# Attention weights turned by fp32 transposes instead of transposed logits; value products a step behind; projections spread evenly over two heads

## The chip, the core and the metric

The kernel runs on one core of a Trainium2 chip. The metric is the device time of one execution in microseconds. The kernel before took 1159.56 us, the median of three runs (1157.66 to 1160.25).

## The reference, cut to what matters

A trunk of two layers over a sequence of 1024 positions with 1024 channels, in float32. Layer 0 is a gated linear recurrence and is not touched here. Layer 1 is attention with a forget gate, 16 heads of 64 channels, causal:

```python
u = h @ w_in                       # q, k, v, gate and one forget logit per head
cum = cumsum(log_sigmoid(f_logit + b_f), axis=1)
logits = (q_blk @ k.T) / sqrt(64) + cum[query] - cum[key]
p = softmax(where(key <= query, logits, -1e30))
o = p @ v
y = (o * silu(gate)) @ w_out       # then the residual sum, and a last RMS norm
```

To hold float32 precision, the kernel splits every matmul operand into a high and a low part (type float32r) and sums three products: high with high, high with low, low with high.

## The kernel before, in words

**Stages.** Layer 0 takes up to some 425 us of the profile. Then come the norm, the first projections, and the attention, head by head, to about 1129 us. The output projection is done in part among heads 13 to 15 (`partial`, whose sums go through DRAM) and ends in `turned`, which turns the stream by fp32 transposes (L850), adds the last two pairs of heads (L854 to L856) and norms.

**One head.** `T[s]` and `U[s]` (`s` is the head's parity) hold k and q with their high and low parts, laid out so that two products give a logit: `T[:, 0]` with `U[:, 0]`, and `T[:, 1]` with `U[:, 1]`, where the second also carries the forget sums. `load` (L559) fills them by DMAs from the projection's tiles `qk`. Two generators then work on a head, each once for each half `c` of the queries:

- `maxima(hd, c)` (L631) makes the logits of 128 queries at a time with queries on the partitions (L654, L655), finds the masked row maximum on DVE (L659), and exponentiates in place in PSUM on ACT (L662), only for the row sums `sums`; the exponentials themselves are thrown away. Its last steps turn the negated maxima (`mrow`, L668) and write them into rows 96 to 99 of `U` (L669), so that the transposed logits come with the maximum subtracted; and they bring the reciprocal sums into row form through DRAM (L680 to L690).
- `weigh(hd, c)` (L701) makes the logits once more, transposed, with keys on the partitions: two key blocks `j` per step, two products each (`ST`, L723 and L724), at least 256 query columns wide. ACT exponentiates out of PSUM into `p` (L729, L732), POOL zeroes the triangle above the diagonal (L737), DVE makes the high part `ph` (L81) and the low part `pl` (L86), and TensorE multiplies both with v into `O` (L757, L758), in the same step. After the last step, ACT and DVE fold the two halves of `O` into `yo` (L762, L763).

`scale` and `gated` (POOL) multiply the output with the gate and the reciprocal sums.

**PSUM.** Eight banks: two buffers of one bank for the tag `g` (projections), two of one bank for `O`, two of two banks for `S`. The logits of `maxima` and the transposed logits of `weigh` both take their tiles from `S`.

**Order.** `run(order, weigh, maxima, fill)` (L786) reads a string: `0` takes a step of `weigh`, `1` a step of `maxima`, and a dot a step of `fill`, the projection for the next pair of heads: six products of 512 columns. A head has two such runs: the first with `weigh(hd, 0)` and `maxima(hd, 1)`, the second with `weigh(hd, 1)` and `maxima(hd + 1, 0)`. `LAG` holds a fill step behind a matmul of a few steps before. In between these edges a planner orders each engine's instructions by its own estimate of when they are ready. `ORDERS` gives even heads (and 12 to 14) 16 dots and the other odd heads 10. In an even head the fill is `kq_units`, k and q of the next pair (16 steps); in an odd head `g_units`, the gate (8 steps). Every fourth head is followed by `values`, products alone. Weights go from DRAM to `wf` (SP queue, L91), their high part is made on ACT (L75) and their low part on POOL (`wl`, L86).

The lines around the change:

Of the kernel before, what the change touches and what calls it, by code (L numbers as in the profile page):

```python
# [17 lines left out]
P = 128  # L18
# [9 lines left out]
ORDERS = (("1.10111.0.10.", "1.1010.1.0.1..10"), (".1101.1..00..11.", "111.0.0.0.11.01...."))  # L28
# [10 lines left out]
def trunk(ctx: ExitStack, tc: tile.TileContext, xt, w0, wg, wo0, pc, gn, gf, w1, wv, wf, bf, wo1, out):  # L39
# [65 lines left out]
    def gemm_steps(ps, pairs, chunks=(slice(0, HALF),)):  # L105

        pairs = list(pairs)
        for cs in chunks:
            o = ps[:, cs]
            for i, ((wh, wl), (xh, xl)) in enumerate(pairs):  # L110
                nc.tensor.matmul(o, wh, xh[:, cs], start=i == 0, stop=False)  # L111
                nc.tensor.matmul(o, wl, xh[:, cs], start=False, stop=False)  # L112
                nc.tensor.matmul(o, wh, xl[:, cs], start=False, stop=i == len(pairs) - 1)  # L113
                if i % 2:
                    yield

# [344 lines left out]
    with ExitStack() as l1:  # L461
# [4 lines left out]
        own = tu.tile([4, 4, P], BF16, name="own")  # L466
        nc.gpsimd.memset(own, 0.0)
        nc.gpsimd.affine_select(
            out=own, in_=own, pattern=[[1, 4], [0, P]], compare_op=ALU.not_equal, fill=1.0, base=0, channel_multiplier=-1
        )  # L470


# [9 lines left out]
        U = [tu.tile([P, 2, SEQ], F32R, tag=f"U{s}", name=f"U{s}") for s in range(2)]  # L482
        for s in range(2):
            nc.gpsimd.memset(f32(T[s][64:, 1]), 1.0)
            nc.vector.memset(f32(U[s][64:, 1]), 0.0)
            nc.vector.memset(f32(U[s][64:68, 1]), -1.0)

        def project(cb_i, use, hs=(0, 1)):

            w = list(weights(w1[cb_i]))  # L490
# [47 lines left out]
        def kq_units(pair, hs=(0, 1)):  # L538

            for is_k in (1, 0):  # L540
                if hs[0] == 0:
                    kq[pair, is_k] = tuple(
                        kqpool.tile([P, SEQ], F32R, tag=f"qk{p}{is_k}", name=f"qk{p}") for p in "hl"
                    )
                hi, lo = kq[pair, is_k]
                eng = nc.vector if pair == 0 else nc.scalar

                def use(h, pt):
                    cs = slice(h * HALF, (h + 1) * HALF)
# [7 lines left out]
                yield from project(is_k * 8 + pair, use, hs)  # L557

        def load(hd, cs=slice(0, SEQ)):  # L559
# [3 lines left out]
            for is_k, A in ((1, T[s]), (0, U[s])):  # L563
                hi, lo = (f32(z[rows, cs]) for z in kq[pair, is_k])
                nc.sync.dma_start(f32(A[:64, 0, cs]), hi)
                if is_k:
                    nc.sync.dma_start(f32(A[:64, 1, cs]), hi)
                    nc.sync.dma_start(f32(A[64:, 0, cs]), lo)
                else:
                    nc.sync.dma_start(f32(A[64:, 0, cs]), hi)  # L570
                    nc.sync.dma_start(f32(A[:64, 1, cs]), lo)
            nc.sync.dma_start(f32(T[s][66:68, 1, cs]), cumd[hd, :, cs])
            nc.sync.dma_start(f32(U[s][64:66, 1, cs]), cumd[hd, :, cs])


        drain(kq_units(0, (0,)))


# [4 lines left out]
        z = at.tile([HEADS, SEQ], F32, tag="p", name="z")  # L583
        e = at.tile([HEADS, SEQ], F32, tag="p", name="e")
# [3 lines left out]
        parts = [at.tile([HEADS, SEQ], F32R, tag=t, name="cp") for t in ("ph", "pl")]  # L588

        def forget(half):  # L590
# [4 lines left out]
            z_, e_, hi, lo = z[:, cs], e[:, cs], *(c[:, cs] for c in parts)  # L595
# [10 lines left out]
            for i in range(2):  # L606
                nc.sync.dma_start(cumd[:, i, cs], f32(parts[i][:, cs]))
            for hd in range(2):
                if half == 0:
                    load(hd, cs)  # L610
# [7 lines left out]
        def g_units(pair):  # L618
# [8 lines left out]
            yield from project(16 + pair, use)  # L627

        stats = {}

        def maxima(hd, c):  # L631

            pair, s = hd // 2, hd % 2
            if c == 0:
                stats[hd] = (
                    at.tile([P, 8], F32R, tag="st", name="st"),  # L640
                    at.tile([P, 8], F32, tag="sums", name="sums"),
                )
            st, sums = stats[hd]
            for i in range(4 * c, 4 * c + 4):
# [4 lines left out]
                qs = slice(i * P, n)  # L649
                for lo_, hi_ in ((0, min(n, HALF - o_)), (HALF - o_, n)):  # L650
# [3 lines left out]
                    nc.tensor.matmul(S[:, lo_:hi_], U[s][:, 0, qs], T[s][:, 0, lo_:hi_], start=True, stop=False)  # L654
# [364 lines left out]
```

## Time and profile before

| | |
|---|---|
| median of the runs | 1159.56 us |
| profiled execution | 1159.8 us, span 1157.9 us |
| TensorE busy | 1131.8 us, 98% of the span |
| VectorE (DVE) busy | 818.3 us, 71% |
| ScalarE (ACT) busy | 590.7 us, 51% |
| GpSimd (POOL) busy | 311.0 us, 27% |
| DMA | 105.41 MB, 31.9% of 16 engines |

A row of a group reads: line, engine, operation, output tile and input tiles, shapes, count, then busy time in us and the mean time of one in ns, then the idle time of the engine just before these instructions and what ended it. A row of the timeline reads: start in us, duration in us, engine, line, operation, tiles, shapes, count, and in brackets the idle time before with its releaser. A row by stretch reads: the stretch, its length, busy time and count of TensorE, of its weight loads, of DVE, ACT and POOL, then the granted clock, the DMA share and GB/s. A row of waits reads: who waited for whom, us in total, how many times, the longest. PEld are TensorE's weight loads. Matmuls are pipelined: the time shown for one is longer than the distance to the next.

### The profile page before, as it was taken

How to read it: one execution, taken by the hardware profiler on the slowest of the kernel's cores; microseconds unless marked ns; L12 is line 12 of the kernel's file. 1: busy time of each engine (PE TensorE's matmuls, PEld its weight loads, DVE VectorE, ACT ScalarE, POOL GpSimd, SP SyncE). 2: the span in 40 equal slices, each digit the busy share in tenths (PEclk: the TensorE clock that was granted, in tenths of full speed). 3: DMA queues.
4: the chain of work that ended last, by engine and by line, in shares of the span. 5: the costliest groups of instructions: out<-in, count | busy, mean ns of one | idle time of the engine just before them, and what ended most of it. 6: DMA issues, size and time to landing. Idle time of an engine off the chain costs nothing.

```text
span 1157.9 us, 15580 instructions
## 1 busy us (share of the span) xinstructions
PE 1131.8 (98%) x5565; PEld 944.8 (82%) x5565; DVE 818.3 (71%) x1294; ACT 590.7 (51%) x1009; POOL 311.0 (27%) x305
## 2 busy tenths in 40 slices
PE   9999999999999999999999999999999999999897
PEld 7787888888888887978888988889888898777685
DVE  7589766677566889556877757777577775577754
ACT  8388345345544656454554545545454454445323
POOL 1212212112021103342332333323333233141310
PEclk9999999999999999999999999999999999999898
DMA  6111111111111124351343323433234331646244
GB/s 211 51 41 50 51 51 55 42 50 41 51 59 37 55 73 151 98 142 38 92 120 92 92 64 92 120 92 83 65 92 110 92 84 60 182 138 202 80 159 182
DMA packets 60221, 105.41 MB, mean 91 GB/s; under 512 B 8744, under 2 KB 23720, under 8 KB 60144
## 3 DMA queue, kind: packets, MB, share of 16 engines
q1 hardware_dynamic: 60144, 104.42, 31.9%
q8 instruction: 44, 0.72, 0.3%
q14 instruction: 33, 0.27, 0.1%
HBM read 63.30 MB, written 15.93 MB: 68 GB/s over the span
## 4 chain that ended last, share of the span: by engine, by line
PE 47%; DVE 5%; ACT 2%; DMA 2%; issue 1%; POOL 1%; DVEq 0%; SPq 0%; ACTq 0%; POOLq 0%
PE gps L111 6%; PE gps L112 6%; PE gps L113 6%; PE O L758 3%; PE ST L723 3%; PE S L655 2%; PE S L654 2%; PE ST L724 2%; PE O L757 2%; PE vps L519 2%; PE vps L517 2%; PE vps L518 2%; DVE pl L86 2%; PE ops L112 1%; PE ops L113 1%
## 5 line engine op out<-in xcount | busy, mean ns | idle before, releaser
L86 POOL TENSOR_TENSOR wl<-wf,wh 128x512 fp32r<-128x512 f32 (+2 forms) x130 | 189.0, 1458 | 504.7 <-ACT wh L75 428.6
L111 PE MATMUL gps<-hh,wh 128*128 128x512 f32 x576 | 226.8, 394 | 1.1 <-DVE qkl L555 0.7
L113 PE MATMUL gps<-hl,wh 128*128 128x512 f32 x576 | 226.7, 394 | 0.0
L112 PE MATMUL gps<-hh,wl 128*128 128x512 f32 x576 | 226.7, 394 | 0.0
L75 ACT CAST wh<-wf 128x512 fp32r<-128x512 f32 (+2 forms) x156 | 94.0, 607 | 140.1 <-PE gps L113 43.1
L662 ACT ACTIVATE S<-S,st 128x128 f32<-128x128 f32 (+7 forms) x128 | 91.4, 714 | 114.0 <-DVE st L659 112.9
L113 PEld LDWEIGHTS gps<-hl,wh 128*128 128x128 f32 x576 | 108.3, 188 | 24.3 <-issue 0.2
L111 PEld LDWEIGHTS gps<-hh,wh 128*128 128x128 f32 x576 | 108.4, 188 | 22.6 <-DVE qkl L555 1.1
L112 PEld LDWEIGHTS gps<-hh,wl 128*128 128x128 f32 x576 | 108.5, 188 | 21.6 <-issue 0.5
L86 DVE TENSOR_TENSOR pl<-p,ph 128x512 fp32r<-128x512 f32 (+2 forms) x130 | 121.7, 953 | 2.3
L81 DVE CAST ph<-p 128x512 fp32r<-128x512 f32 (+2 forms) x130 | 79.2, 619 | 57.0 <-ACT p L729 30.2
L737 POOL TENSOR_SCALAR_AFFINE_SELECT p<-p 128x128 f32<-128x128 f32 (+1 forms) x128 | 47.5, 388 | 201.6 <-ACT p L729 98.1
L659 DVE CUSTOM_DVE_ANT_0 S<-S,mask 128x128 f32<-128x128 f32 (+7 forms) x128 | 96.6, 758 | 7.1 <-PE S L655 6.2
L351 DVE TENSOR_TENSOR x<-x,ops 128x512 f32<-128x512 f32 x80 | 54.0, 681 | 50.7 <-PE ops L113 50.6
L111 PE MATMUL ups<-hh,wh 128*128 128x512 f32 x192 | 76.3, 397 | 2.6 <-DVE us L261 1.9
L113 PE MATMUL ups<-hl,wh 128*128 128x512 f32 x192 | 75.9, 395 | 0.2
L112 PE MATMUL ups<-hh,wl 128*128 128x512 f32 x192 | 75.7, 394 | 0.3 <-POOL wl L86 0.3
L758 PE MATMUL O<-pl,v 128*128 128x512 f32 (+1 forms) x198 | 67.1, 348 | 7.8 <-DVE pl L86 7.8
L729 ACT ACTIVATE p<-ST 128x512 f32<-128x512 f32 (+1 forms) x68 | 53.0, 785 | 42.4 <-PE ST L724 35.5
L518 PE MATMUL vps<-wh,hl 128*128 128x256 f32 (+1 forms) x256 | 72.7, 285 | 0.0
L517 PE MATMUL vps<-wh,hh 128*128 128x256 f32 (+1 forms) x256 | 72.6, 285 | 0.0
L519 PE MATMUL vps<-wl,hh 128*128 128x256 f32 (+1 forms) x256 | 72.4, 284 | 0.0
(192 smaller groups left out, 2517.7 us busy)
## 6 DMA issues: line engine op xcount, KB each, us to landing
wf<-in_w SPq DMA_DIRECT2D x100, 256.0 KB
wf<-in_wo SPq DMA_DIRECT2D x64, 128.0 KB
T<-qkh SPq DMA_DIRECT2D x28, 256.0 KB
U<-qkh SPq DMA_DIRECT2D x28, 256.0 KB
x<-in_xt SPq DMA_DIRECT2D x16, 256.0 KB
x1d<-x SPq DMA_DIRECT2D x16, 256.0 KB
wf<-in_wv SPq DMA_DIRECT2D x16, 256.0 KB
xp<-x1d SPq DMA_DIRECT2D x16, 256.0 KB
```

The source lines that it names most:

```text
L75: nc.scalar.copy(hi, src)
L81: eng.tensor_copy(hi, src)
L86: return eng.tensor_tensor(lo, src, f32(hi), ALU.subtract)
L111: nc.tensor.matmul(o, wh, xh[:, cs], start=i == 0, stop=False)
L112: nc.tensor.matmul(o, wl, xh[:, cs], start=False, stop=False)
L113: nc.tensor.matmul(o, wh, xl[:, cs], start=False, stop=i == len(pairs) - 1)
L517: nc.tensor.matmul(pt, xh, wh, start=k == 0, stop=False)
L518: nc.tensor.matmul(pt, xl, wh, start=False, stop=False)
L519: nc.tensor.matmul(pt, xh, wl, start=False, stop=k == KT - 1)
L659: nc.vector.tensor_tensor_reduce(S[:, :n], S[:, :n], mask[:, SEQ - n :], -1.0, -NEG, ALU.add, ALU.min, accum_out=m)
L662: seen[0] = nc.scalar.activation(S[:, :n], S[:, :n], AF.Exp, bias=f32(m), scale=-1.0, accum_out=sums[:, i : i + 1])
L758: nc.tensor.matmul(o, v, pl[:, jj, : ns[jj]], start=False, stop=j == nj - 1)
```

## The change

The exponentials that `maxima` makes for the row sums are now kept, in eight SBUF tiles `p0` to `p7` (128 queries by as many keys as the triangle needs). `weigh` no longer makes logits: it turns the 128x128 blocks of these tiles on or under the diagonal by fp32 transposes (data stationary, identity moving) into a PSUM tile of the tag `S`. From there ACT makes `ph` and DVE makes `pl` (from the PSUM tile and `ph`), each in tiles of 512 columns with three buffers. The exponential out of PSUM, POOL's triangle, the transposed maxima and their rows in `U` are gone. A block of the diagonal is no longer widened to 256 columns. The products with v of a step are ordered behind the next step's transposes, and those of the last step behind the newest matmul of the fill.

The fill has 12 steps in every head up to 11: k and the first half of q in an even head, the second half of q and the gate in an odd one. Heads 12 to 14 have three dots more in each run, head 15 none. For this, `U` is split into halves: the first half of the queries is one buffer for both parities, the second has one for each; `load` brings k and the asked halves of q, and `late_q` brings the second half of q for the next even head between the two fills. `y` tiles have two buffers in place of three, the residual tiles of `partial` come from another pool, and some tiles at the end and in `forget` are cut or placed anew.

```diff
-ORDERS = (("1.10111.0.10.", "1.1010.1.0.1..10"), (".1101.1..00..11.", "111.0.0.0.11.01...."))
+ORDER = "1.0.1.1.0.1.01", "1.0.1.01.01.0.0"
...
-        U = [tu.tile([P, 2, SEQ], F32R, tag=f"U{s}", name=f"U{s}") for s in range(2)]
+        U0 = tu.tile([P, 2, HALF], F32R, tag="U", name="U")
+        U = [(U0, tu.tile([P, 2, HALF], F32R, tag=f"U{s}", name=f"U{s}")) for s in range(2)]
...
-        def kq_units(pair, hs=(0, 1)):
-            for is_k in (1, 0):
+        def kq_units(pair, parts=((1, (0, 1)), (0, (0, 1)))):
+            for is_k, hs in parts:
...
+                if hs[0] == 0 or pair == 0:
+                    kqw[is_k] = list(weights(w1[is_k * 8 + pair]))
...
+        def load_q(hd, c):
+            s = hd % 2
+            u = U[s][c]
+            hi, lo = (f32(z[s * HD : (s + 1) * HD, halves[c]]) for z in kq[hd // 2, 0])
+            nc.sync.dma_start(f32(u[:64, 0]), hi)
+            nc.sync.dma_start(f32(u[64:, 0]), hi)
+            nc.sync.dma_start(f32(u[:64, 1]), lo)
+            nc.sync.dma_start(f32(u[64:66, 1]), cumd[hd, :, halves[c]])
...
-                m = st[:, i : i + 1]
+                m = at.tile([P, 1], F32, tag="m", name="m", bufs=4)
...
+                p = ps_[i] = at.tile([P, n], F32, tag=f"p{i}", name="p", bufs=1)
                 seen[0] = nc.scalar.activation(
-                    S[:, :n], S[:, :n], AF.Exp, bias=f32(m), scale=-1.0, accum_out=sums[:, i : i + 1]
+                    p, S[:, :n], AF.Exp, bias=m, scale=-1.0, accum_out=sums[:, i : i + 1]
                 )
                 yield
-            pt = ps.tile([P, P], F32, tag="O", name="mrow")
-            nc.tensor.transpose(pt[:4], f32(st[:, 4 * c : 4 * c + 4]), ident)
-            nc.vector.tensor_tensor(
-                U[s][96:100, 1, c * HALF : (c + 1) * HALF].rearrange("p (a b) -> p a b", a=4),
...
+            def products(j0, qlo, parts):
+                for j, q, (ph, pl) in zip((j0, j0 + 1), qlo, parts):
+                    v = V[j][:, 2 * s : 2 * s + 2].rearrange("p a d -> p (a d)")
+                    o = O[:, q - begin :]
+                    nc.tensor.matmul(o, v, ph, start=j == 0, stop=False)
+                    nc.tensor.matmul(o, v, pl, start=False, stop=j == nj - 1)
+            held = None
             for j0 in range(0, nj, 2):
-                A = ps.tile([P, 2, HALF], F32, tag="S", name="ST")
...
+                A = ps.tile([P, 2, HALF], F32, tag="S", name="pt")
+                qlo = [max(begin, j * P) for j in (j0, j0 + 1)]
+                ns = [end - q for q in qlo]
                 for jj in range(2):
-                    q0 = min(max(begin, j * P), end - 256)
-                    nc.tensor.matmul(A[:, jj, :n], T[s][:, 0, ks], U[s][:, 0, q0:end], start=True, stop=False)
...
+                    ks = slice((j0 + jj) * P, (j0 + jj + 1) * P)
+                    for q in range(qlo[jj], end, P):
+                        o = q - qlo[jj]
+                        last[0] = nc.tensor.transpose(A[:, jj, o : o + P], ps_[q // P][:, ks], ident)
+                parts = []
                 for jj in range(2):
...
+                    a = A[:, jj, : ns[jj]]
+                    ph, pl = (at.tile([P, HALF], F32R, tag=t, name=t, bufs=3)[:, : ns[jj]] for t in ("ph", "pl"))
+                    to_hi(ph, a, nc.scalar)
+                    parts.append((ph, pl))
+                for jj, (ph, pl) in enumerate(parts):
+                    to_lo(pl, A[:, jj, : ns[jj]], ph, nc.vector)
+                if held:
+                    with tc.issue_after(last[0].ins):
+                        products(*held)
+                held = j0, qlo, parts
                 yield
+            with tc.issue_after(mm[0].ins):
+                products(*held)
...
-                y = at.tile([P, HALF], F32, tag="xp", name="y", bufs=3)
+                y = at.tile([P, HALF], F32, tag="xp", name="y", bufs=2)
...
             if hd % 2 == 0:
-                if hd < 14:
-                    fill = kq_units(pair + 1)
+                if hd < 12:
+                    fill = kq_units(pair + 1, ((1, (0, 1)), (0, (0,))))
+                elif hd == 12:
+                    fill = chain(kq_units(7), g_units(7))
             elif pair < 6:
-                fill = g_units(pair + 1)
+                fill = chain(kq_units(pair + 1, ((0, (1,)),)), late_q(hd + 1), g_units(pair + 1))
...
-            first, second = ORDERS[hd < 15 and (hd > 11 or hd % 2 == 0)]
+            first, second = (o + "..." * (11 < hd < 15) for o in ORDER)
...
             if hd + 2 < HEADS:
-                load(hd + 2)
+                load(hd + 2, us=(0,) if hd % 2 == 0 and hd < 12 else (0, 1))
```

More of the change, by code (lines that the diff above doesn't have):

```diff
@@ L897, in late @@
                 late_w.append((wh, wl))
-        drain(kq_units(0, (1,)))
+        drain(kq_units(0, ((1, (1,)), (0, (1,)))))
         fill = g_units(0)
@@ L901, in trunk @@
             next(fill)
-        load(0, slice(HALF, SEQ))
-        load(1, slice(HALF, SEQ))
-        run("00.0.00", maxima(0, 0), fill=fill)
+        load(0, halves[1], (1,))
+        load(1, halves[1], (1,))
+        run("00.0.0", maxima(0, 0), fill=fill)
+        load_q(1, 0)
         drain(fill)
```

149 lines of the change are left out of this document (50 added, 99 removed).

## The prediction

> **What bounds the kernel now.** I read the page's engine row and slices first, then the busy times by stretch, then who waited for whom.
>
> ```profile
> span 1157.9 us, 15580 instructions
> PE 1131.8 (98%) x5565; PEld 944.8 (82%) x5565; DVE 818.3 (71%) x1294; ACT 590.7 (51%) x1009; POOL 311.0 (27%) x305
> ...
> 545.00:1072.00 527.00, 521.16 (x2754) 444.88 (x2752) 379.39 (x705) 261.52 (x534) 180.36 (x200) 1.00 0.40 103
> 1072.00:1077.00 5.00, 1.17 (x7) 0.91 (x6) 5.00 (x2) 0.96 (x2) 3.48 (x5) 0.87 0.00 2
> 1077.00:1083.00 6.00, 6.00 (x16) 4.68 (x16) 4.88 (x12) 1.54 (x4) 1.53 (x3) 0.54 0.55 175
> ...
> PE O L758 <- DVE pl L86: 7.8, 5, 3.8
> PEld ST L723 <- ACT S L662: 4.6, 10, 1.7
> ```
>
> TensorE is the bound. In the stretch 545 to 1072, nearly all of the attention, it is busy 521 of 527 us at a granted clock of 1.00; DVE is busy 379 us there and ACT 262 us. So the time is moved by two things only: how long TensorE's own stream is, and the few places where it stands still. The largest such place is the value products' wait for `pl` (7.8 us of TensorE idle in 5 waits, the longest 3.8 us). Behind the longest one the clock is at 0.54 for 6 us, which costs another 6 x 0.46 = 2.8 us.
>
> A matmul's busy time is no price, since records overlap (394 ns is shown for a 512-column one). I price by the distance between starts in an unbroken stream.
>
> ```profile
> 1007.67 0.40 PE L724 MATMUL ST<-U,T 128*128 128x512 f32 x1
> 1007.90 0.34 PE L723 MATMUL ST<-U,T 128*128 128x384 f32 x1
> 1008.08 0.34 PE L724 MATMUL ST<-U,T 128*128 128x384 f32 x1
> ...
> 1121.05 0.28 PE L723 MATMUL ST<-U,T 128*128 128x256 f32 x1
> 1121.17 0.28 PE L724 MATMUL ST<-U,T 128*128 128x256 f32 x1
> 1121.29 0.60 PE L850 MATMUL turn<-ident,x 128*128 128x128 f32 x4
> 1121.65 0.48 PE L854 MATMUL turn<-woh,yhh 128*128 128x512 f32 x1
> 1121.97 0.40 PE L855 MATMUL turn<-woh,yhl 128*128 128x512 f32 x1
> ```
>
> 512 columns take 0.23 us, 384 take 0.18, 256 take 0.12. Four fp32 transposes and the 512-wide product behind them take 1121.97 - 1121.29 = 0.68; less 0.23 that is 0.45, so 0.112 each (the product starts early, but its successor pays for it).
>
> **The change part by part.**
>
> *Transposed logits out.* Per head the kernel makes 12 pairs of ST products.
>
> ```profile
> L724 PE MATMUL ST<-U,T 128*128 128x512 f32 x91 | 35.8, 394 | 0.0
> L724 PE MATMUL ST<-U,T 128*128 128x384 f32 x31 | 10.5, 338 | 0.0
> L724 PE MATMUL ST<-U,T 128*128 128x256 f32 x76 | 19.8, 282 | 0.0
> L668 PE MATMUL mrow<-ident,st 128*4 128x128 f32 x32 | 8.7, 271 | 0.0
> ...
> 577.62 0.27 PE L668 MATMUL mrow<-ident,st 128*4 128x128 f32 x1
> 577.65 0.47 PE L757 MATMUL O<-ph,v 128*128 128x512 f32 x1
> 577.96 0.28 PE L723 MATMUL ST<-U,T 128*128 128x256 f32 x1
> ```
>
> L723 has the same counts, so 182 x 0.23 + 62 x 0.18 + 152 x 0.12 = 41.9 + 11.2 + 18.2 = 71.3 us leave TensorE. The 32 transposes of the row maxima leave too: from 577.62 to 577.96 is 0.34, less 0.23 for the product between, 0.11 each, 3.5 us.
>
> *Transposes in.* A head's causal blocks are 4+3+2+1 = 10 in the first query half and 4x4+10 = 26 in the second: 36. Fifteen heads make 540; head 15 has 10 and, in its quarters, 11 and 15. 576 x 0.112 = 64.5 us come in. They have the operands of the `turn` transposes, data stationary and the identity moving, so I take that price.
>
> The row for one of them is a longer time than the distance: `L850` below shows 10.3 us for 64.
>
> ```profile
> L850 PE MATMUL turn<-ident,x 128*128 128x128 f32 x64 | 10.3, 274 | 2.9 <-ACT sq L860 2.5 <-DMA x<-x1d 0.4
> ```
>
> The Trainium skill (TensorE: Matmul & The Clock Gate, Part 4: PE-mode transpose) gives about 275 ns for a transpose in a kernel's context, and says that transposes do not count as activity for the clock gate. The 274 ns of this row agree as a duration, but starts 0.11 us apart show that it is latency, which overlaps. By the page's figure as a price the transposes would take an estimated 158 us instead of 64.5.
>
> *Narrower products.* The last key block of each query half is no longer widened from 128 to 256 columns: two blocks of `ph` and `pl` per head, three in head 15, 66 products. The trace has no 128-column product of this type. Lower end: the transpose's 0.112, a gain of 0.5 us. Upper end: an ordinary fp32 product, here `rsrow`.
>
> ```profile
> 451.57 1.02 PE L141 MATMUL rsrow<-rs,onesf 128*128 128x512 f32 x2
> 452.02 0.79 PE L423 MATMUL ops<-yh,wh 128*128 128x512 f32 x1
> 452.65 0.40 PE L424 MATMUL ops<-yh,wl 128*128 128x512 f32 x1
> ```
>
> 452.65 - 451.57 - 0.23 = 0.85 us for 512 columns, 0.21 for 128, so 66 x (0.21 - 0.12) = +5.9 us. I take the upper end: these are arithmetic products, accumulated like `rsrow`, and nearer to that row than to a transpose, which only moves data.
>
> TensorE's own stream thus changes by -71.3 - 3.5 + 64.5 + 5.9 = -4.4 us (-10.8 at the lower end).
>
> *The wait for `pl`.* Its cause is in these rows:
>
> ```profile
> L86 DVE TENSOR_TENSOR pl<-p,ph 128x1024 fp32r<-128x1024 f32 x30 | 52.7, 1755 | 0.6
> L659 DVE CUSTOM_DVE_ANT_0 S<-S,mask 128x1024 f32<-128x1024 f32 x16 | 19.6, 1228 | 0.3 <-PE S L655 0.2
> L822 DVE TENSOR_TENSOR xp<-xp,ops 128x512 f32<-128x512 f32 x16 | 10.9, 684 | 4.7 <-PE ops L113 4.7
> ...
> 1069.56 7.00 DVE L86 TENSOR_TENSOR pl<-p,ph 128x1024 fp32r<-128x1024 f32 x1
> ...
> 1069.46 2.39 POOL L699 TENSOR_TENSOR sg<-sg,recb 64x1024 f32<-64x1024 f32 x1 [14.22 <-DMA recb<-recd]
> 1072.30 3.18 POOL L86 TENSOR_TENSOR wl<-wf,wh 128x512 fp32r<-128x512 f32 x3
> ```
>
> `pl` reads two SBUF tensors and takes 1755 ns on average and once 7.00 us, while POOL works through the same stretch. A DVE instruction of that width with a PSUM operand (`S`) takes 1228 ns. In the changed kernel `pl` is made from the PSUM tile and `ph`, like `xp` (684 ns for 512), so I expect 0.69 us with POOL busy or idle. The 79 us of `ph` casts go from DVE to ACT, POOL's triangle selects vanish, and the products stand one step behind their operands. I book the whole stall: -7.8 - 2.8 = -10.6 us. What else could end up late is priced next.
>
> *New waits.* A tile of the S tag (two buffers, shared with the maxima) was free after the exponential; it is now held through two ACT copies and the DVE subtraction.
>
> ```profile
> L729 ACT ACTIVATE p<-ST 128x1024 f32<-128x1024 f32 x30 | 30.4, 1024 | 14.8 <-PE ST L724 14.5 <-issue 0.3
> L75 ACT CAST qkh<-gps 128x512 fp32r<-128x512 f32 x14 | 8.2, 588 | 17.8 <-DVE gps L494 17.5
> L81 DVE CAST ph<-p 128x512 fp32r<-128x512 f32 x69 | 33.9, 492 | 26.5 <-POOL p L737 24.4 <-PE O L758 1.4 <-ACT p L729 0.5
> ```
>
> That is 2 x 0.59 + 0.68 - 1.02 = +0.84 us for a full tile, and about three quarters of it, 0.63, for the mean tile of 768 columns; 96 tiles hold the two buffers 60 us longer, 30 us each. Against it, DVE is freed of the casts, so each of the 128 maxima is served sooner. Lower end: today's weight-load waits for a buffer (4.6 us in 10) vanish. Upper end: none of the 30 us is covered. Now 14 tiles per head share 2 buffers with one projection step (six products, 1.4 us) between most of them, so the queue has slack. I take +3 us, nearest to today's row.
>
> *Moved steps.* Projections: the same products in the same number, 12 steps to each head instead of 16 and 8; only their place changes. They are the cover for all waits above, and the even spread gives the odd heads, where `pl` stalled, four more. U's halves: eight loads a head become T's four and two times four for U; the 0.5 to 1.3 us that each takes on SP lies beside TensorE, half a head ahead of its use. What stands behind `late_q` on SP are the next weights, needed a head later. `y` loads with two buffers and fewer projection steps left for the final quarters (6 against 12): 0 to +6 us; I take +2, as other late work, the final transposed products, can fill there.
>
> The sum: -4.4 - 10.6 + 3 + 2 = -10.0 us. The profiled execution took 1159.8 us (span 1157.9 and 1.9 around it); the runs' median is 1159.6, so both stand for the same kernel, and the forecast is 1149.6, say 1149 us.
>
> **The rivals.**
>
> *Narrow products are cheap and no new wait comes.* -10.8 - 10.6, and up to -4.6 for the old buffer waits: 1134 to 1138. For it: TensorE's stream has hardly any gap but those for `pl`. Against it: the nearest arithmetic row, `rsrow`, prices 128 columns at 0.21.
>
> *The S buffers become the bound (slower).* Place: the first transpose of each step waits until the tile two uses before has passed its subtraction; projections ordered at most three steps ahead run out meanwhile. For it: the hold is 0.63 us longer per tile, and ACT now takes exponentials and copies alike, 12 short copies a head in place of 8 exponentials. Against it: ACT is half idle, DVE loses 80 us. It decides from the point where the mean tile waits (4.4 + 10.6) / 96 = 0.16 us more than now. With 24 of the 30 us uncovered, +24 - 15 + 2: 1171 us; the range of this case is 1162 to 1175.
>
> *The stall only changes its place.* Something else is late, `ph` on a loaded ACT or the last products of each half at the drain, and takes the 10.6 us back: about 1159 us, no change. For it: each half head still ends with a chain from transposes over ACT and DVE to products. Against it: that chain loses POOL and the slow SBUF reads.
>
> *A transpose costs what its record shows.* With 0.27 us each, 576 x 0.16 = +92: 1241 us. Against it: the start distances above. The Trainium skill's 275 ns (TensorE: Matmul & The Clock Gate, Part 4: PE-mode transpose) would give the same.
>
> **How the numbers follow.** Forecast 0.57 (its own range 1142 to 1156), cheap narrow products 0.15, S buffers 0.14, stall only moved 0.11, dear transposes 0.03. A measurement of this kernel tells a change apart from about 0.2%, 2.3 us. Below 1157 lie the first two and a quarter of the fourth: 0.75; within 0.2% half of the fourth and some of the edges: 0.08; slower 0.17. The range 1135 to 1164 leaves out the dear transposes, most of the S-buffer case and the lowest end of the cheap one.
>
> **What will show it.** Transposes about 0.11 us apart in runs, and TensorE's instruction count up by 576 - 396 - 32 = 148. `pl` at about 0.69 us for 512 columns whatever POOL does, and no TensorE wait for `pl` over 1 us. 128-column products 0.21 apart (or 0.11). Waits of the transposes for DVE's subtraction of two tiles before: under 5 us in all if I am right, over 15 us if the S buffers decide. The granted clock at 1.00 between 545 and 1100. I am wrong if TensorE's idle time in the attention is not smaller than now, or if the transposes do not stream.

## The result, and the profile after

The changed kernel takes 1172.88 us (median of 4 runs, 1171.36 to 1174.23) where the kernel before took 1159.05 us on the same chip. The ratio is 1.0119, with a 95% interval of 1.0099 to 1.014. The forecast was 1149 us, a gain; it is a loss of 1.2%.

The page of the changed kernel, its span and engine row:

```profile
span 1169.2 us, 15779 instructions
PE 1123.4 (96%) x5713; PEld 937.4 (80%) x5713; DVE 711.1 (61%) x1202; ACT 591.3 (51%) x1077; POOL 246.8 (21%) x175
```

TensorE is busy 8.4 us less than before (1131.8), DVE 107 us less and POOL 64 us less, and yet the span is 11.3 us longer. The stretches tell where. Here are the stretch from the first logits to 1115 and the rest, of the kernel before and then of the changed one (stretch, length, busy time of TensorE, of its weight loads, of DVE, ACT and POOL, clock, DMA share, GB/s):

```profile
492.00:1115.00 623.00, 611.21 (x3170) 518.89 (x3168) 440.01 (x812) 301.48 (x609) 210.83 (x234) 0.99 0.39 103
1115.00:1158.00 43.00, 33.86 (x191) 27.67 (x188) 20.87 (x43) 16.38 (x46) 2.11 (x4) 0.92 0.48 171
```

```profile
492.60:1115.00 622.40, 592.98 (x3262) 502.69 (x3260) 328.20 (x706) 298.15 (x664) 147.40 (x106) 1.00 0.38 102
1115.00:1169.00 54.00, 42.95 (x245) 35.64 (x244) 25.87 (x55) 20.36 (x59) 4.01 (x4) 0.97 0.46 162
```

In almost the same length TensorE now stands still for 29.4 us instead of 11.8. It gets less far in it: 54 us are left at 1115, before 43. No other engine is near its limit, and the clock is full. What it waits for, by the view of TensorE's waits in the changed kernel:

```profile
PE pt L719 <- ACT p L664: 15.3, 20, 2.4
PE pt L719 <- DVE pl L86: 8.1, 8, 1.1
PE S L654 <- ACT p L664: 3.3, 9, 0.5
PE turn L836 <- ACT sq L846: 2.8, 1, 2.8
PE turn L836 <- DMA x<-x1d: 2.3, 1, 2.3
...
PE O L708 <- DVE pl L86: 0.6, 2, 0.4
```

The old wait of the products for `pl` is all but gone (7.8 to 0.6 us). In its place the transposes `pt` wait 23.4 us in 28 waits, and the logits `S` 3.3 us in 9. One such wait, on TensorE's timeline of the changed kernel, and what DVE and ACT did meanwhile:

```profile
603.39 1.04 PE L719 MATMUL pt<-ident,p 128*128 128x128 f32 x8
604.19 0.47 PE L111 MATMUL gps<-hh,wh 128*128 128x512 f32 x1
...
605.55 0.40 PE L113 MATMUL gps<-hl,wh 128*128 128x512 f32 x1
605.78 0.28 PE L654 MATMUL S<-T,U 128*128 128x256 f32 x1
605.90 0.28 PE L655 MATMUL S<-T,U 96*128 96x256 f32 x1
607.13 1.06 PE L719 MATMUL pt<-ident,p 128*128 128x128 f32 x8 [0.95 <-DVE pl L86]
607.95 0.48 PE L707 MATMUL O<-ph,v 128*128 128x512 f32 x1
608.27 0.40 PE L708 MATMUL O<-pl,v 128*128 128x512 f32 x1
...
604.53 1.07 ACT L75 CAST ph<-pt 128x512 fp32r<-128x512 f32 x2
...
605.72 1.27 DVE L86 TENSOR_TENSOR pl<-pt,ph 128x512 fp32r<-128x512 f32 x2
```

A tile of the S tag is taken at 603.39 and is free again at 606.99, when its second subtraction ends: 3.60 us. In between stand a few projection products and one pair of logits. Then the next transposes stand at the head of TensorE's queue with 0.95 us of idle time, and right behind them, at 607.95, come the products of the step before, which the change orders there. Both copies had ended by 605.60 and the first of the two subtractions halfway to 606.99, so three of the four products had their operands and could have run in the wait; the last needs the second subtraction.

### The profile page after: what moved, and what is told of

Its sections match the earlier page's. It is cut to its first block, busy times and chain, and to the rows that moved or that the text cites. A ratio compares the mean times of both kernels' runs of the same rounds, so it can differ in the third digit from the quotient of the medians.

```text
span 1169.2 us, 15779 instructions
## 1 busy us (share of the span) xinstructions
PE 1123.4 (96%) x5713; PEld 937.4 (80%) x5713; DVE 711.1 (61%) x1202; ACT 591.3 (51%) x1077; POOL 246.8 (21%) x175
## 5 line engine op out<-in xcount | busy, mean ns | idle before, releaser
L86 POOL TENSOR_TENSOR wl<-wf,wh 128x512 fp32r<-128x512 f32 (+2 forms) x130 | 182.8, 1411 | 714.6 <-ACT wh L75 611.8
L664 ACT ACTIVATE p<-S,m 128x128 f32<-128x128 f32 (+7 forms) x128 | 94.9, 741 | 156.1 <-DVE m L659 155.2
L86 DVE TENSOR_TENSOR pl<-pt,ph 128x512 fp32r<-128x512 f32 (+1 forms) x198 | 98.8, 538 | 72.9 <-ACT ph L75 70.8
L75 ACT CAST ph<-pt 128x512 fp32r<-128x512 f32 (+1 forms) x198 | 85.2, 473 | 46.9 <-PE pt L719 42.1
L719 PE MATMUL pt<-ident,p 128*128 128x128 f32 x576 | 81.1, 275 | 23.4 <-ACT p L664 15.3
L719 PEld LDWEIGHTS pt<-ident,p 128*128 128x128 f32 x576 | 65.3, 141 | 36.7 <-ACT p L664 22.7
L707 PE MATMUL O<-ph,v 128*128 128x512 f32 (+1 forms) x198 | 71.2, 360 | 0.0
```

Source lines behind the costliest of these rows:

```text
L75: nc.scalar.copy(hi, src)
L86: return eng.tensor_tensor(lo, src, f32(hi), ALU.subtract)
L664: seen[0] = nc.scalar.activation(p, S[:, :n], AF.Exp, bias=m, scale=-1.0, accum_out=sums[:, i : i + 1])
L707: nc.tensor.matmul(o, v, ph, start=j == 0, stop=False)
L719: last[0] = nc.tensor.transpose(A[:, jj, o : o + P], ps_[q // P][:, ks], ident)
```

## The experiments

Ratios are to the kernel before, which ran beside each experiment on the same chip; its medians there lay between 1155.2 and 1156.3 us. The changed kernel's 1.0119 is from another chip, where the kernel before took 1159.05 us, so ratios are compared and not times. All kernels with transposes issue the same number of matmuls on TensorE (5713), so what differs among them is waiting, and the time at a lower granted clock.

**e1: transposes and logits ordered behind the fill.**

```diff
+                with tc.issue_after(mm[0].ins):
...
+                        nc.tensor.matmul(S[:, lo_:hi_], u[:, 0, qs], T[s][:, 0, lo_:hi_], start=True, stop=False)
...
+                with tc.issue_after(mm[0].ins):
...
+                            last[0] = nc.tensor.transpose(A[:, jj, o : o + P], ps_[q // P][:, ks], ident)
```

> The changed kernel, but the transposes of a weigh step and the logits of a maxima step are ordered behind the newest matmul of the fill, so the fill that the string writes between two users of the S buffers really stands between them. Theory 1 (the two S buffers: a tile is held some 3.6 us from its first transpose to the end of its second subtraction, and the planner puts the next user too close behind): TensorE's waits of transposes and logits for ACT and DVE, 26.7 us in the changed kernel, fall under 10 us, and the time falls by 14 to 22 us to 1151 to 1159. Rival 2 (ACT and DVE together are too slow for the S tiles, wherever the fill stands): the waits move but stay over 20 us, time 1166 to 1176.

Measured: 1.0194 (1.0177 to 1.0212), 1177.63 us, slower than the changed kernel. Waits of TensorE:

```profile
PE pt L721 <- ACT p L665: 15.6, 22, 1.3
PE pt L721 <- DVE pl L86: 10.3, 11, 1.1
PE S L655 <- ACT p L665: 3.7, 11, 0.5
```

29.6 us instead of 26.7: the expectation of theory 1 failed, and the waits are as rival 2 had them (over 20 us), the time a little above its range. In the wait shown above the fill already stood ahead of the transposes, so there the cover was not misplaced but too short. Theory 1's buffers were not refuted by this, its remedy was; rival 2 is answered by e12, where the same engines have the same work and the waits go.

**e2: no subtraction.** The second product takes `ph` again.

```diff
-                    parts.append((ph, pl))
-                for jj, (ph, pl) in enumerate(parts):
-                    to_lo(pl, A[:, jj, : ns[jj]], ph, nc.vector)
+                    parts.append((ph, ph))
```

> The changed kernel without the subtraction: the low part of the turned weights is left out and the second product with v uses the high part again, so TensorE does the same work but an S tile is free after its second ACT copy, 1.2 to 1.4 us earlier. Theory 1 (S buffers): the waits for the subtraction (8.1 us) vanish and those for the exponentials fall too, since DVE is freer: waits 5 to 14 us, time 1155 to 1164. Rival 3 (a transpose waits for its own data, the exponentials of the last maxima): the 15.3 us of waits for ACT's exponentials stay, time 1164 to 1167.

Measured: 0.9988 (0.9977 to 1.0), 1153.67 us.

```profile
PE pt L719 <- ACT p L664: 8.2, 10, 3.2
...
PE S L654 <- ACT p L664: 3.8, 10, 0.5
...
PE pt L719 <- ACT ph L75: 1.8, 3, 0.9
```

The transposes' waits fall from 23.4 to 10.0 us and the kernel gains 1.3% on the changed one, as theory 1 expected; rival 3 is out, as the 15.3 us for ACT's exponentials fall to 8.2. But DVE also does 96 us less here, so the hold and the load are mixed; e15 parts them.

**e3: products in the same step as their transposes.**

```diff
-                if held:
-                    with tc.issue_after(last[0].ins):
-                        products(*held)
-                held = j0, qlo, parts
+                products(j0, qlo, parts)
                 yield
-            with tc.issue_after(mm[0].ins):
-                products(*held)
```

> The changed kernel with the products of a step right behind its own transposes, as in the kernel before. Theory 1: the S waits hardly change, and new waits of the products for the subtraction come on top, if the planner does not fill them: 1172 to 1190. Rival 4 (holding the products back behind the next transposes is what makes TensorE stand still): 1150 to 1164.

Measured: 1.0003 (0.9991 to 1.0015), 1155.89 us. The rival was right and theory 1, as then put, wrong. The waits, and the same place on the timeline as above:

```profile
PE O L707 <- ACT ph L75: 6.0, 12, 0.5
...
PE O L708 <- DVE pl L86: 2.5, 10, 0.3
PE S L654 <- ACT p L664: 2.5, 2, 1.4
...
602.66 0.36 PE L654 MATMUL S<-T,U 128*128 128x256 f32 x1
602.86 0.28 PE L655 MATMUL S<-T,U 96*128 96x256 f32 x1
602.99 0.40 PE L707 MATMUL O<-ph,v 128*128 128x512 f32 x1
603.35 0.50 PE L708 MATMUL O<-pl,v 128*128 128x512 f32 x1
603.68 0.40 PE L707 MATMUL O<-ph,v 128*128 128x512 f32 x1
603.94 0.50 PE L708 MATMUL O<-pl,v 128*128 128x512 f32 x1
604.28 1.03 PE L719 MATMUL pt<-ident,p 128*128 128x128 f32 x8
```

The four products now stand ahead of the next transposes and fill the time until the buffer is free. The transposes hardly wait. This gave theory 6: with two buffers held for 3.6 us, the products of a step are the cover that the next transposes need, and the change orders them behind.

**e4: projections placed as before.** The old strings and the old fill, with the products still held behind.

```diff
-ORDER = "1.0.1.1.0.1.01", "1.0.1.01.01.0.0"
+ORDERS = (("1.10111.0.10.", "1.1010.1.0.1..10"), (".1101.1..00..11.", "111.0.0.0.11.01...."))
...
-                if hd < 12:
-                    fill = kq_units(pair + 1, ((1, (0, 1)), (0, (0,))))
...
+                if hd < 14:
+                    fill = kq_units(pair + 1)
...
-                load(hd + 2, us=(0,) if hd % 2 == 0 and hd < 12 else (0, 1))
+                load(hd + 2)
```

> The changed kernel with the projections placed as before: k and q of the next pair in the even head (16 steps), the gate in the odd one (8), with the order strings of the kernel before. Theory 1: the S tiles are held as long, and the odd heads have less between their users: 1168 to 1185. Rival 5 (the even spread and its strings are what costs): 1145 to 1158.

Measured: 1.0028 (1.0018 to 1.0037), 1158.12 us; the transposes wait 8.9 us, not 23.4. Neither expectation met it, rival 5's by little. The even spread and its strings, which this run doesn't part, are thus a good part of the loss as long as the products are held behind. A reason can be read off the new strings, though no run tests it by itself: the last three transpose steps of the second half stand only one maxima step and one fill step apart.

**e5 and e6: a step behind, but not forced.** In e5 the held products are written ahead of the next transposes (those of the last step keep their order):

```diff
+                if held:
+                    products(*held)
                 for jj in range(2):
...
-                if held:
-                    with tc.issue_after(last[0].ins):
-                        products(*held)
                 held = j0, qlo, parts
```

In e6 they stay behind them, without the two orders:

```diff
                 if held:
-                    with tc.issue_after(last[0].ins):
-                        products(*held)
+                    products(*held)
                 held = j0, qlo, parts
                 yield
-            with tc.issue_after(mm[0].ins):
-                products(*held)
+            products(*held)
```

> The changed kernel with the products still a step behind, but written ahead of the next step's transposes and not ordered behind them. Theory 6 (formed from the order on TensorE: in the changed kernel the products of a step stand behind the next step's transposes, which wait for a free S buffer; ready work queues behind a waiting instruction, while with the products in the same step they stand ahead of it and cover the wait): the transposes' waits fall from 23.4 us to under 8 us, the time to 1150 to 1158 where the kernel before has 1155 to 1160. Rival (a step of delay as such costs, through the buffers of ph and pl or the end of each half): 1162 to 1175.

> The changed kernel with the products a step behind and written behind the next transposes, but without the two orders that hold them there, so that the planner may put them earlier. Theory 6: like the products written first, 1150 to 1160, if the planner sees the waits; 1165 to 1173 if the planner takes the S buffer to be free earlier than it is on the chip and so keeps the transposes ahead.

Measured: e5 1.0023 (1.0008 to 1.0038), 1159.0 us; e6 1.0014 (1.0001 to 1.0027), 1157.52 us. The waits of the transposes are 0.5 us in e5 and 2.5 us in e6, as theory 6 had it; e6's time is in its range and e5's 1 us above. In both the products wait instead for `ph` and `pl`, 8.0 to 8.4 us. (e5's profile is of the longest of its ten executions, 1163.2 us.) So the forced order, not the step of delay, makes the 1%.

**e7: high and low part block by block,** on e3.

```diff
                     to_hi(ph, a, nc.scalar)
+                    to_lo(pl, a, ph, nc.vector)
                     parts.append((ph, pl))
-                for jj, (ph, pl) in enumerate(parts):
-                    to_lo(pl, A[:, jj, : ns[jj]], ph, nc.vector)
```

> The products in the same step, and high and low part made block by block (copy, subtract, copy, subtract) in place of two copies and two subtractions. In the changed kernel all 99 first subtractions start after the second copy, 34 ns behind its end and 0.52 us behind the first one's. If only the order of writing does that, the first subtraction now starts behind the first copy, an S tile is held about 0.5 us less, and the products' waits (8.5 us) fall to 3 to 6 us: 3 to 6 us faster than the same step alone. If reads of one PSUM tile by two engines are kept apart, the second copy waits for the first subtraction, the hold grows, and it is 0 to 10 us slower.

Measured: 1.0242 (1.0201 to 1.0284), 1183.78 us, slower than either expectation in size. The timelines of ACT and DVE in it:

```profile
606.24 0.59 ACT L75 CAST ph<-pt 128x512 fp32r<-128x512 f32 x1 [0.35 <-PE pt L719]
607.59 0.59 ACT L75 CAST ph<-pt 128x512 fp32r<-128x512 f32 x1 [0.76 <-DVE pl L86]
...
606.86 0.69 DVE L86 TENSOR_TENSOR pl<-pt,ph 128x512 fp32r<-128x512 f32 x1 [0.53 <-ACT ph L75]
...
608.26 0.69 DVE L86 TENSOR_TENSOR pl<-pt,ph 128x512 fp32r<-128x512 f32 x1
```

The second copy waits for the first subtraction. The program makes two engines take turns on one PSUM tile, even on different banks of it, so the hold contains all four instructions in whatever order. Here they take 2.71 us from the first copy to the end of the second subtraction (606.24 to 608.95), instead of 2.46 in the changed kernel's tile above. e7 is 2.4% slower than e3, but not all of that is shown to come from the hold: TensorE's idle time grows by 12 us (27.5 to 39.3), and the mean granted clock falls from 0.995 to 0.987, an estimated 10 us more of the 26 us between the two profiled spans.

**e8: the kernel before with the step behind alone,** ordered as in the change; `products` holds the loop that is taken out, and `last` and `mm` the last ST product and fill product, as in the change.

```diff
-                for jj in range(2):
-                    j = j0 + jj
...
+                if held:
+                    with tc.issue_after(last[0].ins):
+                        products(*held)
+                held = j0, qlo, ns, ph, pl
...
+            with tc.issue_after(mm[0].ins):
+                products(*held)
```

> The kernel before with one part of the change alone: the value products a step behind, ordered behind the next step's transposed logits. Theory 6: a tile of transposed logits is free after its exponential, about 1 us after its last product, so the step behind finds a free buffer more often than the transposes do; the waits for pl (7.8 us and the slow clock) go, S waits of 5 to 15 us come: 0.995 to 1.006 of the kernel before. Rival (a step behind always costs what it cost the changed kernel, 17 us against the same step): 1.010 to 1.018.

Measured: 1.0055 (1.0033 to 1.0078), 1162.1 us.

```profile
PE ST L735 <- ACT S L664: 8.4, 8, 2.5
...
PE O L720 <- DVE pl L86: 2.1, 4, 0.8
```

Within theory 6's range: most of the wait for `pl` goes and a wait for a buffer comes, with transposed logits as with transposes. The waits are those of the longest of the ten executions, 1170.9 us at a mean clock of 0.990, so their size is not that of the median.

**e9, e10, e11: one part alone.** e9 is the diff of e3 and that of e4 together, that is the transposes alone; e11 is those of e6 and e4. e10 is the kernel before with the even spread alone (12 steps a head, the second half of q late):

```diff
-ORDERS = (("1.10111.0.10.", "1.1010.1.0.1..10"), (".1101.1..00..11.", "111.0.0.0.11.01...."))
+ORDER = "1.0.1.1.0.1.011", "1.0.1.01.01.01.0"
...
-                if hd < 14:
-                    fill = kq_units(pair + 1)
+                if hd < 12:
+                    fill = kq_units(pair + 1, ((1, (0, 1)), (0, (0,))))
...
```

> The transposes alone: the changed kernel with the products in the same step and the projections placed as before. TensorE's work is 12.2 us less than before, as in all kernels with transposes. Theory 6 (the cost of the changed kernel lies in the products ordered behind the transposes, and grows with the short distances of the new strings): without either, 0.990 to 0.998 of the kernel before. Rival (the longer hold of the S buffers by itself takes the gain back, whatever the order): 1.000 to 1.006.

> The even spread alone: the kernel before, with transposed logits and products in the same step, but with 12 projection steps in every head, the second half of q loaded late, and the new strings (with one more maxima step each, for the turned maxima). Theory 6: the spread costs through short distances between users of the S buffers, less here since a tile of logits is held only to its exponential: 1.000 to 1.006 of the kernel before. If the spread helps the odd heads as such: 0.992 to 0.999.

> The transposes with products a step behind but free to be ordered ahead, and the projections placed as before. Theory 6: the order is not forced, so like the transposes alone, 0.990 to 0.999 of the kernel before.

Measured: e9 1.0063 (1.0047 to 1.0079), e10 1.0354 (1.0334 to 1.0374), e11 1.0024 (1.0014 to 1.0033). All three miss theory 6. e9 comes out just above its rival's range, but not by the rival's mechanism alone: in it the products wait 9.0 us for `pl` (15 waits) and 1.3 us for `ph`, and transposes and logits 5.8 us for buffers: the transposes alone don't bring the work that they save. e10 is by far the slowest; in it logits wait 16.3 us for ACT. It has strings of its own, so it shows that the even spread with these strings doesn't serve the kernel before, and no more. The parts of the change are not additive.

**e12: the short logits out of the S buffers.** The only edit to the changed kernel:

```diff
+                if i < 4:
+                    S = ps.tile([P, HALF], F32, tag="O", name="S")
+                else:
+                    S = ps.tile([P, SEQ], F32, tag="S", name="S")[:, o_:]
-                S = ps.tile([P, SEQ], F32, tag="S", name="S")[:, o_:]
```

> The changed kernel with one thing moved: the maxima's logits of the first query half (at most 512 columns) take their tile from the one-bank tag O, so that in each second run the S buffers serve the transposes alone. Hold, order, strings and engines' work stay. Theory 1 and 6 together (a transpose stands still until an S buffer is free): the waits of the second runs go, about 2 of the 3 us per head, TensorE's waits of transposes fall from 23.4 us to under 12 us and the ratio to the kernel before from 1.012 to between 0.998 and 1.004. If the transposes wait for their own data, or for ACT's and DVE's pace, the ratio stays over 1.008.

Measured: 0.996 (0.9947 to 0.9973), 1150.78 us against 1155.28. It is faster than both kernels, and than expected. Its page and TensorE's waits:

```profile
span 1148.5 us, 15815 instructions
PE 1123.0 (98%) x5713; PEld 939.1 (82%) x5713; DVE 708.7 (62%) x1202; ACT 592.6 (52%) x1077; POOL 247.2 (22%) x175
...
PE S L657 <- ACT p L667: 3.7, 4, 1.5
...
PE O L711 <- DVE pl L86: 2.6, 11, 0.4
...
PE pt L722 <- ACT p L667: 0.8, 1, 0.8
PE pt L722 <- DVE pl L86: 0.8, 1, 0.8
```

The transposes' waits fall from 23.4 us to 1.6 us, though they read the same exponentials and are ordered by the same strings. So they had waited for a buffer and not for their data.

**e13 and e14: the same move elsewhere,** the diff of e12 in e3 and in the kernel before.

> The same move in the kernel with the products in the same step. There the transposes wait hardly at all; what is left are waits of the products for ph and pl (8.5 us) and of the logits for a buffer (2.5 us). Theory 6: a small gain, ratio 0.995 to 1.000. If the O buffers become short instead: 1.002 to 1.010.

> The same move in the kernel before, whose transposed logits wait 4.6 us for an S buffer in all. Theory 1: nothing to gain there, 0.997 to 1.003; a gain of over 0.5% would say that the move helps by something other than the transposes' waits.

Measured: e13 1.0028 (1.0018 to 1.0038), e14 1.0187 (1.0167 to 1.0207). Both miss what theory 6 and theory 1 gave; e13 lies where the expectation has it if the O buffers become short. The move is no gain as such: before, with no transpose to free, it costs 1.9%, with 10.5 us of waits of the products for `ph` and `pl`; why so much is not followed up. In e13 the products in the same step wait 11.6 us for `ph` and `pl`; in e12, a step behind, 2.6 us. Holding them back is worth something as soon as the transposes ahead of them don't stand still.

**e15: a shorter hold with DVE's work unchanged.**

```diff
-                    to_lo(pl, A[:, jj, : ns[jj]], ph, nc.vector)
+                    to_lo(pl, f32(ph), ph, nc.vector)
```

> The changed kernel with the subtraction reading ph twice, out of SBUF, in place of the PSUM tile and ph (the low part is thereby left out of the result, zeros take its place). DVE and TensorE do as many instructions as in the changed kernel, but an S tile is free after its second copy. Theory 1: the hold alone, not DVE's load, made the gain of the kernel without subtraction: transposes' waits under 14 us, ratio 0.998 to 1.005. If DVE's load made it: waits stay over 20 us, ratio 1.008 to 1.014.

Measured: 1.002 (1.0009 to 1.0032), 1158.03 us: the time that theory 1 gave. The waits met neither bound: 18.5 us, 14.9 for ACT's exponentials and 3.6 for its copies. The 8.1 us for the subtraction are gone, though DVE is busier than in the changed kernel (735.6 us against 711.1). The hold alone thus makes most of e2's gain, 1.0 of 1.3%.

**e16 and e17: each ordering part once the cause is removed.** e16 is e12 with the diff of e4, the projections as before; e17 is e12 with that of e6, the products free.

> The changed kernel with the short logits out of the S buffers (as in e12) and the projections placed as before, with the old strings. It tells what the even spread is worth once no transpose waits for a buffer. If the spread then helps, as it does with the products in the same step (1.0003 against 1.0063): 0.998 to 1.004. If the even spread only cost through the S buffers and is worth nothing: 0.994 to 0.997, as e12.

> As e12, but with the products a step behind free to be ordered ahead of the next transposes. With the transposes no longer waiting, the forced order costs nothing and keeps the products off their own operands: the free one is not faster, 0.996 to 1.002 against the 0.996 of e12. If the forced order still costs: under 0.994.

Measured: e16 0.9961 (0.9948 to 0.9974), e17 1.002 (1.0009 to 1.003). The even spread is worth nothing here: with and without it 0.996. In other company it isn't neutral: with the products in the same step it gains 0.6% (e3 against e9), and in the changed kernel it costs 0.9% with its strings (1.0119 against e4's 1.0028). The forced order is worth 0.6% here and costs 1.05% in the changed kernel (1.0119 against e6's 1.0014).

## Why the prediction was wrong, point by point

**TensorE's stream: right, and understated.** Forecast -4.4 us. The transposes stream as priced: in the timeline above eight of them and the next product take 604.50 - 603.39 = 1.11 us, less 0.23, 0.11 each, while a record of one lasts 275 ns on average over the 576. So the rival of dear transposes is out. The Trainium skill (TensorE: Matmul & The Clock Gate, Part 4: PE-mode transpose) gives some 275 ns for one in a kernel's context; the trace agrees with that as a duration and not as a price. The granted clock stayed at 1.00 in the attention. The mis-sized term is the narrow products, of which I took the dear end, 0.21 us:

```profile
622.09 0.28 PE L708 MATMUL O<-pl,v 128*128 128x256 f32 x1
622.21 0.22 PE L707 MATMUL O<-ph,v 128*128 128x128 f32 x1
622.27 0.28 PE L708 MATMUL O<-pl,v 128*128 128x128 f32 x1
622.38 0.95 PE L719 MATMUL pt<-ident,p 128*128 128x128 f32 x7
```

The two 128-column products take 0.06 and 0.11 us to the next start, 0.085 on average against 0.12 for 256 columns. The other 64 are alike: 0.06 on average with `ph`, 0.10 with `pl`. 66 x (0.085 - 0.12) = -2.3 us, where +5.9 was booked. The row that I priced them by, `rsrow`, misled: it is plain float32, and the trace shows two matmul records for each such product of the program (the x2 in that row), one for a float32r product. The stream thus became some 12.6 us shorter.

**The wait for `pl`: right.** It was 7.8 us and is 0.6. The 512-column subtraction takes 683 ns on average (682 where POOL works beside it, 684 where not), and all 198 stay between 278 and 692 ns:

```profile
L86 DVE TENSOR_TENSOR pl<-pt,ph x198: 278/548/692, 522.4 to 1139.0; 128x512 fp32r<-128x512 f32 x91, 128x256 fp32r<-128x256 f32 x43, 128x128 fp32r<-128x128 f32 x33, 128x384 fp32r<-128x384 f32 x31
```

Before, with two SBUF operands, a subtraction of 1024 columns took up to 7.00 us. e15 compares equal widths: there both operands are in SBUF again, and 512 columns take 689 ns where POOL stands still and 893 ns on average where it works, 384 columns up to 1706 ns. The Trainium skill (SBUF — State Buffer, SBUF: two separate sides) calls the port pair that DVE shares with GpSimd an exclusive lock: a DVE instruction with two SBUF inputs and a GpSimd instruction that reads SBUF can't have it together, and the one that starts first holds it for its whole length. The traces agree: these subtractions are late only beside a working POOL, and with one operand in PSUM not even then.

**New waits: the step that failed.** I wrote that "the queue has slack" and took +3 us, "nearest to today's row". The sign that I had named for being wrong came: TensorE's idle time in the attention grew. Measured are 26.7 us of idle time on transposes and logits, against 1.6 on the old ST products. A wait costs somewhat more than its idle time: in the one shown, the product ahead starts at 605.90 and takes some 0.12 us, so the transposes would have started at 606.02 and did at 607.13, 1.11 later with 0.95 of idle. If the other 36 cost 0.16 us more as well, an estimate from this one, that is 6 us, and 31 more than before in all. It takes back the 12.6 us of stream and the 10.0 us of the stall (7.2 us of waits, 2.8 of the slow clock) and 8 more; with 2.2 us of longer waits in `turn` this accounts for most of the 11.3 us of the span.

The rival "the S buffers become the bound" had 0.14 and gave 1171 us with a range of 1162 to 1175; of the cases named it is the one that came, at 1172.9. That its number is so close is in part luck: it took 24 us of uncovered waits against 15 us of gains, and some 31 came against 23. Its sign, over 15 us of waits for the subtraction, didn't come: those are 8.1 us, and 15.3 of the 23.4 us are for ACT's exponentials, which it doesn't name.

What I had wrong is, first, the hold. I counted two copies and one subtraction for a full tile, 2 x 0.59 + 0.68 = 1.86 us, as if the other subtraction ran beside the second copy. In the tile shown above it is 2.46 us from the first copy to the end of the second subtraction (604.53 to 606.99), since the two engines take turns; so it is 0.6 us more than the 0.84 us that I added. Second, the cover. I counted on the projection step between two tiles, and put the step of delay down as a gain ("the products stand one step behind their operands"), without asking what is queued behind a transpose that waits: exactly those products, 0.9 us long and mostly ready. That this order makes the loss is what e3, e5 and e6 show, and that it does so only while the buffers are short is what e12 shows. I also read the strings only for their number of dots and not for the distance from one transpose step to the next, which is one maxima step and one fill step at two places in the second half's string. The waits that end with ACT's exponential are waits for a buffer too. One such wait:

```profile
616.46 0.55 PE L719 MATMUL pt<-ident,p 128*128 128x128 f32 x3 [0.64 <-ACT p L664]
...
615.63 0.69 ACT L664 ACTIVATE p<-S,m 128x512 f32<-128x512 f32 x1 [1.05 <-DVE m L659]
...
615.46 1.15 DVE L86 TENSOR_TENSOR pl<-pt,ph 128x512 fp32r<-128x512 f32 x2
```

These transposes are the last step of a head's second half and read its last exponentials, over 800 columns wide; the one that released them is 512 wide, of the next head's first half. So they didn't wait for their data. The other buffer's tile is read by the subtraction until 616.61, later than they start; what the exponential freed is the S tile of its logits. e12 bears this out.

**Moved steps.** "The even spread gives the odd heads four more" was booked at nothing beyond the stall. Once no transpose waits for a buffer that is right (e16 against e12); in the changed kernel it is wrong, where the spread costs 0.9% with its strings (e4) and so belongs to the failed step. For the end of the kernel +2 us were booked, and the waits in `turn` are 5.1 us instead of 2.9; whether the `y` loads make them, no run tells.

**The stall only changes its place, dear transposes, cheap narrow products.** The first named other chains than the one that came; the second is refuted; the third was right in its price and wrong in that "no new wait comes".

What stays open: why e9, the transposes alone, wait 9 us for `pl` where the kernel before waited 7.8 with slower subtractions. It may be that the planner puts the products too close behind there, but no run separates its estimate from the strings.

## What to carry to other kernels

Where an engine keeps its order, as TensorE does in these timelines, ready work behind a waiting instruction waits too. Work that is ordered behind an instruction that may wait for a buffer can no longer cover that wait; do it only when the buffer is free by then, and find out by the distance from one user of the buffers to the next, not by their average. When a PSUM tile changes from one reader to a chain of two engines, recount the hold of its slot against that distance, and look first for users of the same buffers that fit elsewhere: here moving the short logits alone took the changed kernel from 1.0119 to 0.996.

## What the runs showed of the hardware that was not expected

A float32r product of 128 columns is not dearer than one of 256: 0.06 to 0.11 us to the next start against 0.12. In the wait shown above the transposes came 0.16 us later than the idle time before them tells. With both operands in SBUF a 512-column subtraction took 689 ns beside an idle POOL and 893 ns on average beside a working one; with one operand in PSUM it took 684 and 682 ns. And the kernel's time is far more sensitive to the order around two PSUM buffers than to the work: with the same products on TensorE, e12 and the changed kernel lie 1.6% apart, while all of the work saved is 1.1%.
